# Opening part of a decoder trunk: adapter mixes in one VectorE operation, later splits on VectorE, three squares and six roundings on ScalarE

## The chip, the core and the metric

One core of one Trainium2 chip runs the whole kernel. The metric is device time of one execution in microseconds (us). Names of engines as the profile has them: PE is TensorE's matmul stream (PEld its weight loads), DVE is VectorE, ACT is ScalarE, POOL is GpSimd, SP is SyncE, which issues the loads. In the profile, L513 is line 513 of the kernel before.

## What is computed

Two decoder layers on x of 512 tokens by 1024 channels. The opening part, which the change touches, belongs to the first layer:

```python
h = rms_norm(x, norm_g[l, 0])
xx = jnp.pad(x, ((0, 0), (1, 0), (0, 0)))[:, :-1] - x
xr, xw, xk, xv, xa, xg = [x + xx * mu[i] for i in range(6)]
r = xr @ w_rkv[0]
k = xk @ w_rkv[1]
w = -jax.nn.softplus(-(w_decay0 + jnp.tanh(xw @ w_decay1) @ w_decay2)) - 0.5
a = jax.nn.sigmoid(a0 + (xa @ a1) @ a2)
g = jax.nn.sigmoid(xg @ g1) @ g2
kk = heads(k * k_k)
kk = kk * lax.rsqrt(jnp.maximum(jnp.sum(kk * kk, axis=-1, keepdims=True), 1e-24))
```

After it come the recurrence, its output projection, a convolutional feed-forward, attention with a window of 128, and a second feed-forward.

## The kernel before

Channels lie on partitions: x is eight tiles of 128 channels by 512 tokens, often worked in two halves of 256. Large products run in three passes: a weight is rounded to a high part (`whi`) and the rest is kept as a low part (`wlo`), the input likewise (two tiles both named `h`), and PE adds high by high, high by low and low by high. So each operand needs a rounding (a cast) and a subtraction.

The opening is written out by hand. The string `START` is a list of steps; each word is a step's letter, its chunk and, where there is a choice, its engine (D is DVE, A is ACT, P is POOL). Each engine works its own steps in the order of the list, and a step waits for what it reads and for the buffer that it writes. Twelve buffers of 512 columns (`t2`) serve most of the steps. The steps that matter here, with their lines:

- `x` (L442): normalises a half chunk. `m`, `s` (L337, L342): its mix for k. `c`, `u` (L452, L455): high and low part of that mix; PE's products `a`, `b`, `k` and `C` (L473) read them.
- `h`, `l` (L463, L466): high and low part of a weight block of 128 by 1024.
- `d` (L508, L509): the difference to the token before, one tile of 512 columns for each chunk. From it come the mixes for r (number 0), the decay (1), the adapter of a (4) and the gate (5): either `M` (L513), one DVE operation (difference times mu plus x), or the pair `e` (L517, a scaling on ACT) and `f` (L520, an addition on POOL). Each chunk needs four; sixteen of the 32 go as `e` and `f`.
- `W` (L525) and `g` (L532): PE's products of the adapters and the gate, which read these mixes as fp32.
- `H`, `L` (L616, L619): high and low part of the mix for r.
- `o` (L491) and `y` (L494): k scaled by k_k, and k itself, out of PSUM. `z` (L499 on ACT, L501 on POOL): the square of the scaled k, into a single buffer `ksq`. `S` (L504): PE's sum of squares.
- `E` (L587 to L611): loads, roundings and low parts of the adapters' second weights, in two column halves. The roundings stand on DVE (L591, L598, L605), the subtractions on POOL (L593, L600, L607).

Later stages are put in order by a scheduler when the program is built. After about 113 us the opening's end follows (tables of ScalarE, the norm of k), then a loop over eight blocks of r.

Of the kernel before, what the change touches and what calls it, by code (L numbers as in the profile page):

```python
# [12 lines left out]
F32 = mybir.dt.float32  # L13
F32R = mybir.dt.float32r
U32 = mybir.dt.uint32
AF = mybir.ActivationFunctionType
ALU = mybir.AluOpType
# [10 lines left out]
VQ = 4  # L28
VP = 3
VY = 1  # L30
START = 'q00P q02A q03D G02 O +023D q01P G03 G00 G01 +002D +001D q06P q05A q07D G07 q04P G05 +067P G06 +045D h0A n0 G04 l0P q12D q10A q11D G10 q13D +101D t0 G11 v0 h1D T0 l1D +123P G12 r2 G13 B0 q14A x02P +102D q16A r3 1 q15A x07D x03P q17A x00D m02 +145D +167P m00 x01D s02 m03 +146P s00 m01 s03 x04P c02A n1 c00A c03A s01 x06D t1 c01A u03D u00P m07 u02P m04 v1 u01D T1 h2A x05P s04 a000 x10D a010 x11D h3A a020 l2P d0D a030 c04A M50 b000 m06 a021 s07 m11 b010 s06 m05 g0 s11 u04P c07A r4 G15 c06D u06D l3P c11A a001 s05 b020 G17 c05D a040 G14 u05D b030 e10 u11D x14D a031 m10 a112 x15D m14 x17D d1P a050 r5 u07D m15 s14 b040 m17 c14D a060 B1 s15 G16 f10 a070 u14D e11 a061 a071 s10 s17 b050 e41 f11 M40 b060 c17A b041 c15A c10D b021 u17D b112 e01 f41 u15D u10D b142 e00 e51 f51 b011 x16P a142 4 x13P a051 m16 a152 s16 x12P m13 a041 b152 c16A s13 d2P m12 c13D W0 u13D s12 c12D W1 u16P u12D e42 M12 d3P e02 a172 M52 b070 a122 f42 M43 e53 b061 e03 b122 f53 a011 a132 a162 f00 b102 f01 a102 b031 o0 y0D g1 f02 z0A h5D h4A b051 M13 W2 l5P y1A r6 b071 b172 d4P r7 b162 b132 o1 l4D b001 W3 d5P M14 e04 S0 2 E30 o2 y3D o3 g2 z1P k5 M44 y2A f03 E40 E50 f04 M54 e45 f45 W4 h6D o5 l6D S1 e15 E60 k4 z2P f15 E70 g3 E80 E00 h7D o4 y4A y5D r8 l7D g4 d6P E10 S2 E31 C0 z3A C1 E20 W5 H0A E01 L0P e46 M55 E41 f46 e16 S3 H1D C2 E11 E61 L1D z4A f16 C3 H2A E51 L2D C4 H3A M56 H4A M06 C5 M05 E71 d7P L3D E21 S4 C6 z5A H5D E81 M47 e57 L5D C7 f57 M17 H6D W6 L4D h8A y7D y6D M07 g5 l8P o7 o6 S5 H7D W7 z6A L7D S6 F4 g6 z7P F5 E9 L6P F0 S7 g7 N0 F1 F2 N1 F3 R0 5 J00 Z0 N2 R2 A00 Z1 V30 A01 V00 V20 V31 R1 V01 V10 V21 J10 Y V32 V11 J01 N3 V02 R3 V22 R5 X0 R4 N4 V12 N5 R6 X1 R7 J11'
FIRST = 'apib0c1drs'
RG0 = 0
RG1 = 1
# [42 lines left out]
class Net:  # L77
# [272 lines left out]
    def rwkv(self, after_pool):  # L350
        nc, tc, d, par = self.nc, self.tc, self.d, self.par
        X = self.X
# [17 lines left out]
        t2 = lambda name, dt=F32: pT.tile([128, T], dt, name=name, tag="t2")  # L370
        mu = par[:, PC["mu"]:PC["mu"] + 48]
# [8 lines left out]
        raws, W, P, R = {}, {}, {}, {}  # L380
        ss, pwa, pg = self.ps(), None, None
        sq, st, ms, mw, df, rsb = {}, {}, {}, {}, {}, {}
# [129 lines left out]
            mw[i, c] = t2("m")  # L512
            nc.vector.scalar_tensor_tensor(mw[i, c], df[c], mu[:, 8 * i + c:8 * i + c + 1], X[:, c], ALU.mult, ALU.add)  # L513

        def f_e(i, c):
            mw[i, c] = t2("m")
            nc.scalar.activation(mw[i, c], df[c], AF.Identity, scale=mu[:, 8 * i + c:8 * i + c + 1])  # L517

        def f_f(i, c):
            nc.gpsimd.tensor_tensor(mw[i, c], mw[i, c], X[:, c], ALU.add)  # L520

        def f_W(c):
            R["wa"] = pwa = R.get("wa") or self.ps()
            for i, x in enumerate((mw.pop((1, c)), mw.pop((4, c)))):
                nc.tensor.matmul(pwa[64 * i:64 * i + 64, :], one["wa1"][:, c, 64 * i:64 * i + 64], x, start=c == 0, stop=c == 7, skip_group_check=True)  # L525
# [58 lines left out]
        def f_E(i, n=0):  # L584
            ns = slice(n * T, n * T + T)
            A2, AL, W2, WL = (one[k] for k in ("A2", "AL", "W2", "WL"))
            if i == 0:  # L587
                R["a2"] = t2("a2r")
                nc.sync.dma_start(R["a2"], d["a2"][:, ns])
            elif i == 1:  # L590
                nc.vector.tensor_copy(A2[:, ns], R["a2"])  # L591
            elif i == 2:
                nc.gpsimd.tensor_tensor(AL[64:128, ns], R["a2"][64:128, :], A2[64:128, ns].bitcast(F32), ALU.subtract)  # L593
            elif i == 3:
                R["w2"] = t2("w2r")
                nc.sync.dma_start(R["w2"], d["w2"][:, ns])
            elif i == 4:
                nc.vector.tensor_copy(W2[:, ns], R["w2"])  # L598
            elif i == 5:
                nc.gpsimd.tensor_tensor(WL[0:64, ns], R["w2"][0:64, :], W2[0:64, ns].bitcast(F32), ALU.subtract)  # L600
            elif i == 6:
                R["w2l"] = t2("w2l")
                nc.sync.dma_start(R["w2l"], d["w2l"][:, ns])
            elif i == 7:
                nc.vector.tensor_copy(WL[64:128, ns], R["w2l"][64:128, :])  # L605
            elif i == 8:
                nc.gpsimd.tensor_tensor(WL[96:128, ns], R["w2l"][96:128, :], WL[96:128, ns].bitcast(F32), ALU.subtract)  # L607
            else:
                one0 = t2("one0")
                nc.gpsimd.memset(one0[64:128, :], 1.0)  # L610
                nc.vector.tensor_copy(one["TB"][64:128, :], one0[64:128, :])  # L611
# [84 lines left out]
        with tc.manual_schedule():  # L696
            for k in START.split():
                fs[k[0]](*(int(x) if x.isdigit() else x for x in k[1:]))
# [55 lines left out]
        for q in range(8):  # L754
# [6 lines left out]
            for n in range(4):  # L761
                ns = slice(n * 128, n * 128 + 128)
# [58 lines left out]
        E0, n0, s0 = self.inverse(0, sp0, sp0)  # L821
        E1, n1, s1 = self.inverse(1, pE, sp0)
# [734 lines left out]
```

## Time and profile before

| what | value |
|---|---|
| median of three runs | 1413.12 us (1409.84 to 1417.49) |
| profiled execution | 1420.08 us, span in the trace 1418.2 us |
| PE busy | 1335.7 us, 94% |
| DVE busy | 940.0 us, 66% |
| ACT busy | 653.3 us, 46% |
| POOL busy | 528.9 us, 37% |

Busy shares are means over stages with different limits. Times below are counted from the span's start. The granted clock (PEclk) is the share of TensorE's full speed: 1.00 is 2.4 GHz, 0.50 is 1.2 GHz.

### The profile page before, as it was taken

To read this page: it belongs to the slowest core of one execution; us is meant where nothing else is said; L and a number is where in the kernel's file an instruction comes from. 1 tells how busy PE (TensorE), PEld (TensorE's weight loads), DVE (VectorE), ACT (ScalarE), POOL (GpSimd) and SP (SyncE) were. 2 spreads that over 40 slices of the span, in tenths; PEclk is the share of its full clock that TensorE was granted. 3 is DMA by queue.
4 is the path that set the end of the run, shared out by engine and by line. 5 is a ranking of instruction groups with operands and counts; after the bars stand their busy time and mean duration, and the time that the engine had idled before them with its cause. 6 is when DMAs were issued, how large, how long until landed. Compare 5 with 4: busy or idle time off the path is not lost.

```text
span 1418.2 us, 26067 instructions
## 1 busy us (share of the span) xinstructions
PE 1335.7 (94%) x10840; PEld 1116.4 (79%) x10840; DVE 940.0 (66%) x1384; ACT 653.3 (46%) x1192; POOL 528.9 (37%) x335
## 2 busy tenths in 40 slices
PE   4889999877989999999999989999999999999996
PEld 4766778777889888888888989766888888888886
DVE  8787898764797497776612287886658777763214
ACT  6436541334666454434322467766635444433232
POOL 6773420002445244333312635424533343332144
PEclk9899999898999999999999989999999999999998
DMA  5122121002344223333233424212323233232333
GB/s 198 38 69 72 60 63 35 14 19 63 107 153 146 89 76 104 104 97 97 82 97 93 138 96 150 89 60 74 120 71 108 90 103 104 89 99 83 95 99 122
DMA packets 43591, 130.07 MB, mean 92 GB/s; under 512 B 4560, under 2 KB 12496, under 8 KB 43472
## 3 DMA queue, kind: packets, MB, share of 16 engines
q1 hardware_dynamic: 41072, 126.11, 28.4%
q10 hardware_dynamic: 2400, 2.29, 0.5%
q8 instruction: 85, 1.39, 0.4%
q14 instruction: 34, 0.28, 0.1%
HBM read 124.19 MB, written 2.10 MB: 89 GB/s over the span
## 4 chain that ended last, share of the span: by engine, by line
PE 63%; DVE 3%; ACT 1%; issue 1%; POOL 0%; DVEq 0%; ACTq 0%; POOLq 0%
PE ps L124 19%; PE ps L126 19%; PE ps L125 19%; PE ps L1394 2%; PE ps L1358 1%; PE ps L1357 1%; DVE h L198 1%; DVE X L210 1%; DVE wlo L107 1%; PE ps L1384 1%; ACT h L197 1%; DVE acc L173 0%; PE ps L154 0%; POOL wlo L107 0%; DVE yy L209 0%
## 5 line engine op out<-in xcount | busy, mean ns | idle before, releaser
L107 POOL TENSOR_TENSOR wlo<-raw,whi 128x1024 fp32r<-128x1024 f32 (+1 forms) x126 | 304.3, 2417 | 350.6 <-ACT whi L102 304.9
L102 ACT CAST whi<-raw 128x1024 fp32r<-128x1024 f32 (+1 forms) x215 | 219.5, 1025 | 333.8 <-PE ps L125 235.3
L125 PE MATMUL ps<-h,whi 128*128 128x512 f32 (+1 forms) x984 | 359.7, 366 | 3.0 <-DVE h L198 2.9
L126 PE MATMUL ps<-h,wlo 128*128 128x512 f32 (+1 forms) x984 | 359.5, 366 | 2.8 <-DVE wlo L107 1.8
L124 PE MATMUL ps<-h,whi 128*128 128x512 f32 (+1 forms) x984 | 360.1, 368 | 0.0
L107 DVE TENSOR_TENSOR wlo<-raw,whi 128x1024 fp32r<-128x1024 f32 (+1 forms) x89 | 117.9, 1325 | 174.2 <-ACT whi L102 174.0
L126 PEld LDWEIGHTS ps<-h,wlo 128*128 128x128 f32 x984 | 189.2, 192 | 34.8 <-DVE wlo L107 2.7
L125 PEld LDWEIGHTS ps<-h,whi 128*128 128x128 f32 x984 | 189.3, 192 | 34.0 <-DVE h L198 3.5
L124 PEld LDWEIGHTS ps<-h,whi 128*128 128x128 f32 x984 | 188.1, 192 | 33.8 <-issue 2.8
L125 PE MATMUL ps<-g,whi 128*128 128x512 f32 (+1 forms) x440 | 153.7, 349 | 0.0
L124 PE MATMUL ps<-g,whi 128*128 128x512 f32 (+1 forms) x440 | 153.4, 349 | 0.0
L126 PE MATMUL ps<-g,wlo 128*128 128x512 f32 (+1 forms) x440 | 153.4, 349 | 0.0
L303 POOL TENSOR_TENSOR cs<-cs 128x512 f32<-128x512 f32 x44 | 57.7, 1312 | 242.8 <-DVE cs L295 200.3
L143 DVE TENSOR_TENSOR g<-cs,g 128x512 fp32r<-128x512 f32 x44 | 93.9, 2134 | 40.8 <-ACT g L142 40.8
L173 DVE TENSOR_TENSOR acc<-acc,sq 128x256 f32<-128x256 f32 x56 | 48.8, 886 | 72.9 <-ACT sq L172 72.6
L124 PEld LDWEIGHTS ps<-g,whi 128*128 128x128 f32 x440 | 82.6, 188 | 12.2
L125 PEld LDWEIGHTS ps<-g,whi 128*128 128x128 f32 x440 | 82.6, 188 | 12.2
L126 PEld LDWEIGHTS ps<-g,wlo 128*128 128x128 f32 x440 | 82.6, 188 | 12.1
L302 ACT ACTIVATE cs<-cs 128x512 f32<-128x512 f32 x44 | 27.8, 632 | 120.8 <-DVE cs L295 120.8
L292 DVE TENSOR_TENSOR rp<-ps,rsx 128x512 f32<-128x512 f32 x88 | 59.7, 686 | 31.3 <-PE ps L126 31.3
L293 ACT ACTIVATE cs<-rp,par 128x512 f32<-128x512 f32 x88 | 70.3, 812 | 16.3 <-DVE g L143 8.6
L294 DVE SCALAR_TENSOR_TENSOR cs<-rp,par,cs 128x511 f32<-128x511 f32 x88 | 74.0, 847 | 1.9 <-ACT cs L293 1.9
(298 smaller groups left out, 2404.8 us busy)
## 6 DMA issues: line engine op xcount, KB each, us to landing
raw<-w_up SPq DMA_DIRECT2D x88, 512.0 KB, 3.5
raw<-w_down SPq DMA_DIRECT2D x40, 512.0 KB, 3.6
raw<-w_or SPq DMA_DIRECT2D x16, 512.0 KB, 3.7
raw<-w_q SPq DMA_DIRECT2D x16, 512.0 KB, 3.5
raw<-w_oa SPq DMA_DIRECT2D x16, 512.0 KB, 3.5
raw<-w_down SPq DMA_DIRECT2D x20, 384.0 KB, 3.2
raw<-w_k SPq DMA_DIRECT2D x8, 512.0 KB, 3.7
raw<-w_r SPq DMA_DIRECT2D x8, 512.0 KB, 3.7
```

The costliest lines, as they stand in the source:

```text
L102: (nc.vector.tensor_copy if lo and lo[-1] == "v" else nc.scalar.copy)(hi, raw)
L107: (nc.gpsimd if lo[0] == "P" else nc.vector).tensor_tensor(wl, raw, hi.bitcast(F32), ALU.subtract)
L124: mm(p, hi, ah, start=first, stop=False, skip_group_check=True)
L125: mm(p, hi, al, start=False, stop=False, skip_group_check=True)
L126: mm(p, lo, ah, start=False, stop=last, skip_group_check=True)
L143: self.nc.vector.tensor_tensor(lo, src, hi.bitcast(F32), ALU.subtract)
L173: (eng or nc.vector).tensor_tensor(acc[:, o:o + n], acc[:, o:o + n], sq, ALU.add)
L292: nc.vector.tensor_tensor(r, p, rsx, ALU.mult)
L293: nc.scalar.activation(c, r, AF.Identity, bias=par[:, cb:cb + 1], scale=par[:, cw + 88:cw + 89])
L294: nc.vector.scalar_tensor_tensor(c[:, 1:], r[:, :T - 1], par[:, cw + 44:cw + 45], c[:, 1:], ALU.mult, ALU.add)
L303: nc.gpsimd.tensor_tensor(cs[:, 0], cs[:, 0], cs[:, 1], ALU.mult)
L1394: self.nc.tensor.matmul(po[64 * h:64 * h + 64, :], self.V[:, n - o, 64 * kvh:64 * kvh + 64], pt[:, o].rearrange("a i q -> a (i q)"), start ...
```

## The change

Sixteen mixes leave the pair `e` (ACT) and `f` (POOL) and become `M` (DVE), each at the place in the list where its `f` stood. Two low parts of weights (`l5`, `l8`) and two of the mix for r (`L0`, `L6`) go from POOL to DVE. Three squares (`z1`, `z2`, `z7`) go from POOL to ACT. In `E` the six roundings go from DVE to ACT, the six subtractions from POOL to DVE. SP's loads keep their order.

```diff
-b020 G17 c05D a040 G14 u05D b030 e10 u11D x14D a031
+b020 G17 c05D a040 G14 u05D b030 u11D x14D a031
...
-G16 f10 a070 u14D e11 a061 a071 s10 s17 b050 e41 f11 M40
+G16 M10 a070 u14D a061 a071 s10 s17 b050 M11 M40
...
-l5P
+l5D
...
-        def f_e(i, c):
-            mw[i, c] = t2("m")
-            nc.scalar.activation(mw[i, c], df[c], AF.Identity, scale=mu[:, 8 * i + c:8 * i + c + 1])
-
-        def f_f(i, c):
-            nc.gpsimd.tensor_tensor(mw[i, c], mw[i, c], X[:, c], ALU.add)
-
...
-                nc.vector.tensor_copy(A2[:, ns], R["a2"])
+                nc.scalar.copy(A2[:, ns], R["a2"])
             elif i == 2:
-                nc.gpsimd.tensor_tensor(AL[64:128, ns], R["a2"][64:128, :], A2[64:128, ns].bitcast(F32), ALU.subtract)
+                nc.vector.tensor_tensor(AL[64:128, ns], R["a2"][64:128, :], A2[64:128, ns].bitcast(F32), ALU.subtract)
...
```

The other two pairs of `E` change in the same way. Line numbers of the changed kernel are 7 lower from L520 on.

POOL, from the difference of chunk 1 to the half chunks 6, 3 and 2 of the second half of the tokens (L442). Before:

```order
L508 TENSOR_TENSOR df<-X 128x511
L509 TENSOR_SCALAR df<-X 128x1
L520 TENSOR_TENSOR m<-m,X 128x512 x4
L442 TENSOR_TENSOR X<-X,rsb 128x256 x3
L508 TENSOR_TENSOR df<-X 128x511
```

After:

```order
L508 TENSOR_TENSOR df<-X 128x511
L509 TENSOR_SCALAR df<-X 128x1
L442 TENSOR_TENSOR X<-X,rsb 128x256 x3
L508 TENSOR_TENSOR df<-X 128x511
L509 TENSOR_SCALAR df<-X 128x1
```

The four additions that stood ahead of the three normalisations are gone.

DVE in the same stretch, around the low parts of the k mix (L455). Before:

```order
L455 TENSOR_TENSOR h<-m,h 128x256
L342 SCALAR_TENSOR_TENSOR m<-X,par,m 128x256 x2
L513 SCALAR_TENSOR_TENSOR m<-df,par,X 128x512
L452 CAST h<-m 128x256
L455 TENSOR_TENSOR h<-m,h 128x256 x3
L650 TENSOR_SCALAR hpar<-par 128x8
```

After:

```order
L513 SCALAR_TENSOR_TENSOR m<-df,par,X 128x512
L455 TENSOR_TENSOR h<-m,h 128x256
L342 SCALAR_TENSOR_TENSOR m<-X,par,m 128x256 x2
L513 SCALAR_TENSOR_TENSOR m<-df,par,X 128x512 x2
L452 CAST h<-m 128x256
L455 TENSOR_TENSOR h<-m,h 128x256
L513 SCALAR_TENSOR_TENSOR m<-df,par,X 128x512
L455 TENSOR_TENSOR h<-m,h 128x256 x2
L513 SCALAR_TENSOR_TENSOR m<-df,par,X 128x512
L643 TENSOR_SCALAR hpar<-par 128x8
```

Four mixes have come in, three of them ahead of the second of the three low parts.

DVE at the end of the products of k, up to the last two copies of k out of PSUM (L494). Before:

```order
L605 CAST WL<-w2l 64x512
L619 TENSOR_TENSOR h<-m,h 128x512
L616 CAST h<-m 128x512
L513 SCALAR_TENSOR_TENSOR m<-df,par,X 128x512
L619 TENSOR_TENSOR h<-m,h 128x512
L513 SCALAR_TENSOR_TENSOR m<-df,par,X 128x512
L616 CAST h<-m 128x512
L619 TENSOR_TENSOR h<-m,h 128x512
L494 COPY bk<-ps 128x8x64 x2
L513 SCALAR_TENSOR_TENSOR m<-df,par,X 128x512
```

After (L609 is the cast and L612 the subtraction of the mix for r, L600 a subtraction of `E`):

```order
L609 CAST h<-m 128x512
L600 TENSOR_TENSOR WL<-w2l,WL 32x512
L513 SCALAR_TENSOR_TENSOR m<-df,par,X 128x512
L612 TENSOR_TENSOR h<-m,h 128x512
L513 SCALAR_TENSOR_TENSOR m<-df,par,X 128x512 x2
L609 CAST h<-m 128x512
L612 TENSOR_TENSOR h<-m,h 128x512
L494 COPY bk<-ps 128x8x64 x2
L513 SCALAR_TENSOR_TENSOR m<-df,par,X 128x512
```

The two copies keep their place behind the mixes of the last chunks; one more mix stands ahead of them.

## Rows read from the trace of the kernel before

**Rows 1.** The page, busy time: us, share of the span, instructions of each engine.

```profile
PE 1335.7 (94%) x10840; PEld 1116.4 (79%) x10840; DVE 940.0 (66%) x1384; ACT 653.3 (46%) x1192; POOL 528.9 (37%) x335
```

**Rows 2.** PE in order of time: start, us, operation [idle before, who ended it].

```profile
51.07 0.42 PE L473 MATMUL ps<-h,whi 128*128 128x256 f32 x1 [2.90 <-DVE h L452]
52.47 0.58 PE L473 MATMUL ps<-h,whi 128*128 128x256 f32 x1 [0.98 <-DVE h L455]
...
105.61 1.73 PE L525 MATMUL ps<-m,wa 128*64 128x512 f32 x4 [4.06 <-DVE m L513]
109.13 2.08 PE L504 MATMUL ps<-ksq,cst 128*128 128x512 f32 x2 [1.78 <-ACT ksq L499]
111.00 2.10 PE L532 MATMUL ps<-g,m 128*128 128x160 f32 x8
```

**Rows 3.** Stretches: us, busy time and (instructions) by engine, granted clock, DMA, GB/s.

```profile
35.40:106.40 71.00, 63.05 (x327) 48.19 (x326) 56.51 (x59) 27.38 (x45) 53.67 (x43) 0.93 0.17 54
51.30:58.10 6.80, 5.82 (x27) 5.63 (x27) 6.18 (x4) 0.72 (x1) 5.63 (x4) 0.50 0.00 0
105.90:112.70 6.80, 5.02 (x13) 2.54 (x10) 5.31 (x8) 5.12 (x8) 1.35 (x2) 0.50 0.55 162
120.00:180.00 60.00, 60.00 (x273) 45.44 (x271) 48.05 (x58) 32.05 (x52) 28.74 (x23) 1.00 0.19 60
180.00:240.00 60.00, 57.97 (x937) 45.48 (x939) 57.22 (x103) 20.05 (x29) 7.45 (x6) 1.00 0.16 48
```

**Rows 4.** DVE by line, 35.4 to 106.4: busy us, mean ns | idle before, releasers.

```profile
L513 DVE SCALAR_TENSOR_TENSOR m<-df,par,X 128x512 f32<-128x512 f32 x14 | 19.4, 1408 | 4.6 <-POOL h L619 3.5 <-POOL df L509 1.1
L466 DVE TENSOR_TENSOR wlo<-raw,whi 128x1024 fp32r<-128x1024 f32 x3 | 9.2, 3078 | 0.1
L342 DVE SCALAR_TENSOR_TENSOR m<-X,par,m 128x256 f32<-128x256 f32 x7 | 5.3, 765 | 2.8 <-ACT m L337 2.8
...
L455 DVE TENSOR_TENSOR h<-m,h 128x256 fp32r<-128x256 f32 x7 | 4.4, 650 | 0.1
...
L452 DVE CAST h<-m 128x256 fp32r<-128x256 f32 x4 | 3.0, 748 | 0.1
...
L494 DVE COPY bk<-ps 128x512 f32<-128x512 f32 x3 | 2.0, 682 | 2.8 <-ACT ar L491 2.8
L598 DVE CAST W<-w2r 128x512 fp32r<-128x512 f32 x2 | 1.9, 974 | 1.4 <-DMA w2r<-w 1.4
...
L605 DVE CAST WL<-w2l 64x512 fp32r<-64x512 f32 x2 | 1.6, 788 | 0.1
```

**Rows 5.** DVE in order of time, where POOL did little; columns as in rows 2.

```profile
36.37 0.29 DVE L452 CAST h<-m 128x256 fp32r<-128x256 f32 x1
36.58 0.48 DVE L342 SCALAR_TENSOR_TENSOR m<-X,par,m 128x256 f32<-128x256 f32 x1
...
41.06 1.08 DVE L455 TENSOR_TENSOR h<-m,h 128x256 fp32r<-128x256 f32 x3
...
94.06 2.07 DVE L513 SCALAR_TENSOR_TENSOR m<-df,par,X 128x512 f32<-128x512 f32 x3
...
108.28 1.21 DVE L107 TENSOR_TENSOR wlo<-raw,whi 128x1024 fp32r<-128x1024 f32 x1
```

**Rows 6.** POOL by line, 35.4 to 106.4; columns as in rows 4.

```profile
L520 POOL TENSOR_TENSOR m<-m,X 128x512 f32<-128x512 f32 x16 | 23.3, 1474 | 6.3 <-ACT m L517 6.2
L508 POOL TENSOR_TENSOR df<-X 128x511 f32<-128x511 f32 x6 | 8.2, 1371 | 3.0 <-DVE m L513 2.9
...
L509 POOL TENSOR_SCALAR df<-X 128x1 f32<-128x1 f32 x6 | 3.0, 504 | 0.0
...
L442 POOL TENSOR_TENSOR X<-X,rsb 128x256 f32<-128x256 f32 x3 | 2.4, 819 | 0.0
```

**Rows 7.** ACT in order of time, between the last copies of k and their squares' sum.

```profile
107.13 1.29 ACT L491 ACTIVATE ar<-ps,par 128x512 f32<-128x512 f32 x2 [6.40 <-DVE bk L494]
108.45 0.63 ACT L499 ACTIVATE ksq<-ar 128x512 f32<-128x512 f32 x1
```

More of the change, by code (lines that the diff above doesn't have):

```diff
@@ L30 @@
 VY = 1
-START = 'q00P q02A q03D G02 O +023D q01P G03 G00 G01 +002D +001D q06P q05A q07D G07 q04P G05 +067P G06 +045D h0A n0 G04 l0P q12D q10A q11D G10 q13D +101D t0 G11 v0 h1D T0 l1D +123P G12 r2 G13 B0 q14A x02P +102D q16A r3 1 q15A x07D x03P q17A x00D m02 +145D +167P m00 x01D s02 m03 +146P s00 m01 s03 x04P c02A n1 c00A c03A s01 x06D t1 c01A u03D u00P m07 u02P m04 v1 u01D T1 h2A x05P s04 a000 x10D a010 x11D h3A a020 l2P d0D a030 c04A M50 b000 m06 a021 s07 m11 b010 s06 m05 g0 s11 u04P c07A r4 G15 c06D u06D l3P c11A a001 s05 b020 G17 c05D a040 G14 u05D b030 e10 u11D x14D a031 m10 a112 x15D m14 x17D d1P a050 r5 u07D m15 s14 b040 m17 c14D a060 B1 s15 G16 f10 a070 u14D e11 a061 a071 s10 s17 b050 e41 f11 M40 b060 c17A b041 c15A c10D b021 u17D b112 e01 f41 u15D u10D b142 e00 e51 f51 b011 x16P a142 4 x13P a051 m16 a152 s16 x12P m13 a041 b152 c16A s13 d2P m12 c13D W0 u13D s12 c12D W1 u16P u12D e42 M12 d3P e02 a172 M52 b070 a122 f42 M43 e53 b061 e03 b122 f53 a011 a132 a162 f00 b102 f01 a102 b031 o0 y0D g1 f02 z0A h5D h4A b051 M13 W2 l5P y1A r6 b071 b172 d4P r7 b162 b132 o1 l4D b001 W3 d5P M14 e04 S0 2 E30 o2 y3D o3 g2 z1P k5 M44 y2A f03 E40 E50 f04 M54 e45 f45 W4 h6D o5 l6D S1 e15 E60 k4 z2P f15 E70 g3 E80 E00 h7D o4 y4A y5D r8 l7D g4 d6P E10 S2 E31 C0 z3A C1 E20 W5 H0A E01 L0P e46 M55 E41 f46 e16 S3 H1D C2 E11 E61 L1D z4A f16 C3 H2A E51 L2D C4 H3A M56 H4A M06 C5 M05 E71 d7P L3D E21 S4 C6 z5A H5D E81 M47 e57 L5D C7 f57 M17 H6D W6 L4D h8A y7D y6D M07 g5 l8P o7 o6 S5 H7D W7 z6A L7D S6 F4 g6 z7P F5 E9 L6P F0 S7 g7 N0 F1 F2 N1 F3 R0 5 J00 Z0 N2 R2 A00 Z1 V30 A01 V00 V20 V31 R1 V01 V10 V21 J10 Y V32 V11 J01 N3 V02 R3 V22 R5 X0 R4 N4 V12 N5 R6 X1 R7 J11'
@@ new lines @@
+START = 'q00P q02A q03D G02 O +023D q01P G03 G00 G01 +002D +001D q06P q05A q07D G07 q04P G05 +067P G06 +045D h0A n0 G04 l0P q12D q10A q11D G10 q13D +101D t0 G11 v0 h1D T0 l1D +123P G12 r2 G13 B0 q14A x02P +102D q16A r3 1 q15A x07D x03P q17A x00D m02 +145D +167P m00 x01D s02 m03 +146P s00 m01 s03 x04P c02A n1 c00A c03A s01 x06D t1 c01A u03D u00P m07 u02P m04 v1 u01D T1 h2A x05P s04 a000 x10D a010 x11D h3A a020 l2P d0D a030 c04A M50 b000 m06 a021 s07 m11 b010 s06 m05 g0 s11 u04P c07A r4 G15 c06D u06D l3P c11A a001 s05 b020 G17 c05D a040 G14 u05D b030 u11D x14D a031 m10 a112 x15D m14 x17D d1P a050 r5 u07D m15 s14 b040 m17 c14D a060 B1 s15 G16 M10 a070 u14D a061 a071 s10 s17 b050 M11 M40 b060 c17A b041 c15A c10D b021 u17D b112 M41 u15D u10D b142 M51 b011 x16P a142 4 x13P a051 m16 a152 s16 x12P m13 a041 b152 c16A s13 d2P m12 c13D W0 u13D s12 c12D W1 u16P u12D M12 d3P a172 M52 b070 a122 M42 M43 b061 b122 M53 a011 a132 a162 M00 b102 M01 a102 b031 o0 y0D g1 M02 z0A h5D h4A b051 M13 W2 l5D y1A r6 b071 b172 d4P r7 b162 b132 o1 l4D b001 W3 d5P M14 S0 2 E30 o2 y3D o3 g2 z1A k5 M44 y2A M03 E40 E50 M04 M54 M45 W4 h6D o5 l6D S1 E60 k4 z2A M15 E70 g3 E80 E00 h7D o4 y4A y5D r8 l7D g4 d6P E10 S2 E31 C0 z3A C1 E20 W5 H0A E01 L0D M55 E41 M46 S3 H1D C2 E11 E61 L1D z4A M16 C3 H2A E51 L2D C4 H3A M56 H4A M06 C5 M05 E71 d7P L3D E21 S4 C6 z5A H5D E81 M47 L5D C7 M57 M17 H6D W6 L4D h8A y7D y6D M07 g5 l8D o7 o6 S5 H7D W7 z6A L7D S6 F4 g6 z7A F5 E9 L6D F0 S7 g7 N0 F1 F2 N1 F3 R0 5 J00 Z0 N2 R2 A00 Z1 V30 A01 V00 V20 V31 R1 V01 V10 V21 J10 Y V32 V11 J01 N3 V02 R3 V22 R5 X0 R4 N4 V12 N5 R6 X1 R7 J11'
@@ L597, in f_E @@
             elif i == 4:
-                nc.vector.tensor_copy(W2[:, ns], R["w2"])
+                nc.scalar.copy(W2[:, ns], R["w2"])
             elif i == 5:
-                nc.gpsimd.tensor_tensor(WL[0:64, ns], R["w2"][0:64, :], W2[0:64, ns].bitcast(F32), ALU.subtract)
+                nc.vector.tensor_tensor(WL[0:64, ns], R["w2"][0:64, :], W2[0:64, ns].bitcast(F32), ALU.subtract)
             elif i == 6:
@@ L604, in f_E @@
             elif i == 7:
-                nc.vector.tensor_copy(WL[64:128, ns], R["w2l"][64:128, :])
+                nc.scalar.copy(WL[64:128, ns], R["w2l"][64:128, :])
             elif i == 8:
-                nc.gpsimd.tensor_tensor(WL[96:128, ns], R["w2l"][96:128, :], WL[96:128, ns].bitcast(F32), ALU.subtract)
+                nc.vector.tensor_tensor(WL[96:128, ns], R["w2l"][96:128, :], WL[96:128, ns].bitcast(F32), ALU.subtract)
             else:
```

## The prediction

> **What bounds the kernel now.** I read the page first: PE is busy 94% of the span [rows 1], so a gain has to come from PE's idle time or from its slow clock. The chain of work that ended last doesn't reach back to the opening, so there I read PE in order of time and looked at who ended each idle piece. From 120 us to 180 us PE is busy for all of 60 us, and from 180 us to 240 us for 57.97 [rows 3]: what the opening saves is passed on by these stages. In the opening PE stops in three places after its start. The first, near 33 us, lies ahead of the first step that moves. The second is 2.90 + 0.98 us, for DVE's high and low part of the k mix (L452, L455). The third is 4.06 us for a mix (L513) and 1.78 us for the last but one square (L499) [rows 2]. After the second and the third the granted clock is 0.50, the lower of TensorE's two levels (1.2 GHz of 2.4): 5.82 us and 5.02 us of PE's work were done in that state [rows 3] and would take half at full clock, so it costs 2.9 and 2.5 us. All that PE can get back is 2.90 + 0.98 + 4.06 + 1.78 + 2.9 + 2.5 = **15.1 us**.
>
> DVE is the engine PE waits for, and DVE is late because of POOL. In 35.4 to 106.4 DVE is busy 56.51 of 71.0 us [rows 3], but the same operation takes different times. A mix (L513) takes 2.07 / 3 = 0.69 us where POOL is nearly idle [rows 5] and 1.41 us in the mean [rows 4]; a low part of a weight 1.21 against 3.08. The copy that reads PSUM (L494) has a mean of 0.68 and shows no such spread [rows 4]. So operations with all operands in SBUF wait inside their own time for POOL. What this costs in the stretch, mean rows [rows 4] against free rows [rows 5]: mixes 19.4 - 14 x 0.69 = 9.7; weight low parts 9.2 - 3 x 1.21 = 5.6; k mixes (L342) 5.3 - 7 x 0.48 = 1.9; low parts (L455) 4.4 - 7 x 0.36 = 1.9; casts (L452) 3.0 - 4 x 0.29 = 1.8. Together **20.9 us**.
>
> **The change part by part, on DVE, up to its two copies of k at 106.42** (the wait on DVE's L494 in [rows 7]). Added: sixteen mixes at 0.69 are 11.0 us; one weight low part 1.2 (the other stands behind the copies); six subtractions of `E` and one low part for r (the other also stands behind) at the mix's 0.69, 4.8. Removed: six casts of `E`; L598's pair took 1.9, L605's 1.6 [rows 4], and the third pair, of L598's shape, as much as that: 5.4. Net **+11.6 us** of work.
>
> What POOL keeps in the stretch: six differences, 8.2 + 3.0, and three normalisations, 2.4 [rows 6], with one low part of about 0.8 (a normalisation's mean) 14.4 of its 53.67 us [rows 3], or 27%. If DVE's waits shrink with POOL's work, 73% of 20.9 goes, **-15.3 us**. DVE's idle time for POOL, 3.5 + 1.1 [rows 4], goes too, **-4.6**: the low part that it waited for is now its own or comes from an emptier POOL. The idle time for PE, ACT, DMA stays as it is. The sum is 11.6 - 15.3 - 4.6 = **-8.3 us** at the copies.
>
> Behind the copies stands a chain that doesn't change: two scalings on ACT (1.29), the square (0.63), then PE's sum of squares at 109.13 [rows 7, 2]. PE must be there too: without its stops and the slow clock after 51 it comes 2.90 + 0.98 + 2.9 + 4.06 + 1.78 = 12.6 us earlier. It gets one new stop: three added mixes stand ahead of the second of three low parts (at 41.06 before [rows 5]), 2.1 us, and the three normalisations, which now run beside them, can hold DVE 2.4 us more. Up to 4.3 us of this the DVE chain hides, 12.6 - 8.3; all of it would be 4.5. So DVE decides, at -8.3.
>
> Then the clock. The sum of squares and the gate's products after it take 2.08 and 2.10 us at 0.50 [rows 2]; with PE's idle time before them cut to under 3 us I expect full clock, -2 us. Bounds: 0 and -2.5.
>
> At no cost: ACT loses sixteen scalings and gets three squares and six casts, and it is busy 27.38 of 71.0 us [rows 3]. A square on ACT takes 0.63 [rows 7], and `ksq`, a single buffer, is free as soon as PE has read it. The casts of `E` are first read after 113 us. If ACT's cover fails, each late square costs PE up to 0.6. POOL gets nothing. SP's queue is the same, and loads follow buffers that come free earlier. Some rows of later stages change places by one or two; I take 0, bounds -1 and +1.
>
> The sum: -8.3 - 2 = -10.3, taken as **-10 us**. The profiled execution took 1420.08, of which 1418.2 is the span: it becomes 1410. It lies 7 us above the median of the runs shown; the stops of the opening are no reason for that difference, so the same step is taken from the median: 1413.1 - 10 = **1403**.
>
> **What the notes say of it.** L513 takes 0.69 or 1.41 as POOL is idle or busy, L494 always 0.68 [rows 4, 5]. The Trainium skill, SBUF — State Buffer, Who interferes with whom, says that a VectorE instruction with two SBUF inputs, and casts in the two-port modes, share a port pair with GpSimd, that the one that starts first holds it for its whole instruction, and that one with at most one SBUF input outside these modes doesn't contend: the trace agrees on L494. The rule weighs against a part of my sum, since by it every POOL operation that is left can hold DVE for its full time (rival 2). The Trainium skill, Perfetto Trace Analysis, Optimizing Scalar/DVE Operations, says that a saturated VectorE is a reason to move work off it, even to GpSimd, and adds that their common port may make this useless. This change does the opposite (rival 3).
>
> **The rivals.**
> 1. *All of it.* DVE's loss goes wholly and its 2.8 us for the mixes behind POOL's normalisations too: 11.6 - 20.9 - 4.6 - 2.8 = -16.7 at the copies, which is more than PE can use. PE is the bound and saves its 15.1: 1398. For it: the sixteen additions, 23.3 us of POOL's time [rows 6], go, and the normalisations come right behind a difference. Against: six differences stay. 0.12.
> 2. *What POOL keeps holds DVE fully.* Each of its 14.4 us is then lost on DVE, so only 20.9 - 14.4 = 6.5 goes: 11.6 - 6.5 - 4.6 = +0.5, no gain at the copies; perhaps 3 us at the second stop and its clock. In between lies a mixed case with half of this, about -5: 1408 to 1412. Against: before, 53.67 us of POOL cost 20.9, or 0.39 for each us, which makes 5.6 of 14.4. For: DVE has fewer gaps now, so that POOL's operations more often meet one. 0.20.
> 3. *DVE becomes the bound, slower.* If the long times are not POOL's doing, nothing of 20.9 goes: 11.6 - 4.6 = +7.0 at the copies, and PE's longer stop at 105 us adds one more piece of slow clock, 2: +9, or 1422. It decides as soon as less than a third (7.0 us) of the loss goes. Against: L494 and the free rows. 0.06.
> 4. *The gain doesn't arrive.* From 180 us to 240 us DVE is busy 57.22 of 60 [rows 3] and PE can't go ahead of it. But DVE comes there earlier too, since its own queue is what got shorter; DMA's share there is 0.16. Price -2 or so: 1411. 0.04.
>
> **How the numbers follow.** My forecast has 0.58, with -7 to -13 (the part of the loss that goes between 0.65 and 0.9, the clock between 0 and -2.5): 1400 to 1406. A measurement of this kernel can tell about 0.5%, 7 us, from no change. Faster by more than that: nearly all of the forecast, rival 1 and a little of rival 2, 0.71. Within it: most of rival 2, rival 4, a rest of the forecast, 0.23. Slower: rival 3, 0.06. The range is **1397 to 1412**: it leaves out the far end of rival 1 and rival 3, and part of rival 2.
>
> **What the profile after would show.** Mixes (L513) with a mean near 0.8 instead of 1.41, weight low parts near 1.3; DVE busy some 50 to 53 us up to its copies of k, and these at about 98. PE's stop at 51 us gone or under 1 us, one of 1 to 3 us near 43 us, the 4.06 us for the mix gone, 1 to 3 us left for the square, the clock 1.00 around the third place. The loop over r starts 10 us earlier and everything after it is shifted by as much. I am wrong if the mixes stay above 1.1 us, if PE waits for a mix at all in the third place, or if the shift is there at 120 us and not at 240.

## The result and the profile after

The kernel after takes **1398.8 us** (median of 6 runs, 1394.94 to 1407.97), the kernel before took 1415.78 on the same chip: ratio 0.990, 95% interval 0.986 to 0.993. Timed twice more in later sessions it took 1403.4 (10 runs; before 1413.6; 0.992, 0.989 to 0.996) and 1404.7 (6 runs; before 1416.9; 0.991, 0.987 to 0.994). Forecast were 1403 and 10 us less than before; measured are 17.0, 10.2 and 12.2 us less. The profiled execution took 1400.81 us, its span is 1398.9.

The page, busy time by engine, answering [rows 1]:

```profile
PE 1322.9 (95%) x10840; PEld 1104.3 (79%) x10840; DVE 934.7 (67%) x1404; ACT 647.6 (46%) x1185; POOL 488.2 (35%) x306
```

What ended PE's idle time from 24 us to 125 us: engine, line, us in total, times, longest:

```profile
PE ps L473 <- DVE h L455: 1.4, 1, 1.4
PE ps L473 <- ACT h L452: 1.3, 1, 1.3
PE ps L504 <- ACT ksq L499: 1.0, 1, 1.0
...
```

The first two are the stop near 33 us, ahead of the change. The stops at 51 us and at 105 us [rows 2] are gone; of the third place only the wait for the square is left. There PE in order of time (start, us, operation [idle before, who ended it]), then ACT ([rows 7] before):

```profile
96.09 1.08 PE L518 MATMUL ps<-m,wa 128*64 128x512 f32 x4
98.17 1.12 PE L504 MATMUL ps<-ksq,cst 128*128 128x512 f32 x2 [1.00 <-ACT ksq L499]
99.13 1.25 PE L525 MATMUL ps<-g,m 128*128 128x160 f32 x8
```

```profile
96.17 1.29 ACT L491 ACTIVATE ar<-ps,par 128x512 f32<-128x512 f32 x2 [2.05 <-DVE bk L494]
97.49 0.63 ACT L499 ACTIVATE ksq<-ar 128x512 f32<-128x512 f32 x1
```

L518 is L525 of before: the adapter's products no longer wait for a mix. The scalings, the square and the sum of squares all stand 10.96 us earlier (107.13, 108.45, 109.13 before). The sum takes 1.12 us instead of 2.08, the gate's products 1.25 instead of 2.10.

Stretches (us, busy and instructions of PE, PEld, DVE, ACT, POOL, then the granted clock, DMA, GB/s). The first goes up to DVE's last two copies of k, so that it answers the 71.0 us of [rows 3]; the last answers 180 us to 240 us there, since this work now stands some 11 us earlier:

```profile
35.40:95.40 60.00, 60.00 (x323) 46.93 (x323) 49.98 (x77) 21.99 (x39) 16.82 (x17) 0.95 0.19 62
34.20:45.00 10.80, 10.30 (x63) 10.30 (x64) 10.77 (x22) 3.50 (x9) 5.65 (x5) 0.69 0.01 3
170.00:230.00 60.00, 58.00 (x945) 44.85 (x944) 55.66 (x102) 18.52 (x26) 6.29 (x5) 0.97 0.16 47
```

DVE does more instructions in less time: 77 in 49.98 us against 59 in 56.51. Where this comes from, DVE by line from 35.4 to 95.4 (busy us, mean ns | idle before, releaser), against [rows 4]:

```profile
L513 DVE SCALAR_TENSOR_TENSOR m<-df,par,X 128x512 f32<-128x512 f32 x30 | 22.0, 770 | 0.0
L466 DVE TENSOR_TENSOR wlo<-raw,whi 128x1024 fp32r<-128x1024 f32 x4 | 5.6, 1427 | 0.1
L342 DVE SCALAR_TENSOR_TENSOR m<-X,par,m 128x256 f32<-128x256 f32 x7 | 4.9, 723 | 0.0
L612 DVE TENSOR_TENSOR h<-m,h 128x512 fp32r<-128x512 f32 x6 | 4.1, 688 | 2.7 <-ACT h L609 2.6
L455 DVE TENSOR_TENSOR h<-m,h 128x256 fp32r<-128x256 f32 x7 | 3.8, 553 | 0.1
...
L586 DVE TENSOR_TENSOR AL<-a2r,A 64x512 fp32r<-64x512 f32 x2 | 2.1, 1054 | 0.1
...
L600 DVE TENSOR_TENSOR WL<-w2l,WL 32x512 fp32r<-32x512 f32 x2 | 1.4, 689 | 0.2
L593 DVE TENSOR_TENSOR WL<-w2r,W 64x512 fp32r<-64x512 f32 x2 | 1.4, 682 | 3.5 <-ACT W L591 3.5
L609 DVE CAST h<-m 128x512 fp32r<-128x512 f32 x3 | 1.3, 421 | 0.0
L452 DVE CAST h<-m 128x256 fp32r<-128x256 f32 x4 | 1.2, 291 | 0.1
...
```

Thirty mixes take 22.0 us where fourteen took 19.4. How far the opening as a whole moved is seen at its last product of r (L473). One row has all matmuls of a line: ns min/median/max, the first and the last start in us. Before, then after:

```profile
L473 PE MATMUL ps<-h,whi x206: 278/389/799, 23.6 to 123.5; 128*128 128x256 f32 x63, 128*128 128x512 f32 x40
```

```profile
L473 PE MATMUL ps<-h,whi x206: 279/389/799, 23.7 to 111.0; 128*128 128x256 f32 x63, 128*128 128x512 f32 x40
```

The **last start of L473**, 123.5 and 111.0, is the mark used below: the opening is 12.5 us shorter.

### The profile page after: what moved, and what is told of

It is laid out like the page before. It is cut to its first block, busy times and chain, and to the rows that moved or that the text cites. A ratio compares the mean times of both kernels' runs of the same rounds, so it can differ in the third digit from the quotient of the medians.

```text
span 1398.9 us, 26032 instructions
## 1 busy us (share of the span) xinstructions
PE 1322.9 (95%) x10840; PEld 1104.3 (79%) x10840; DVE 934.7 (67%) x1404; ACT 647.6 (46%) x1185; POOL 488.2 (35%) x306
## 4 chain that ended last, share of the span: by engine, by line
PE 64%; DVE 4%; issue 1%; ACT 1%; POOL 0%; DVEq 0%; ACTq 0%; POOLq 0%
PE ps L124 19%; PE ps L126 19%; PE ps L125 19%; PE ps L1387 2%; PE ps L1351 1%; PE ps L1350 1%; DVE h L198 1%; DVE X L210 1%; DVE wlo L107 1%; PE ps L1377 1%; DVE acc L173 0%; PE ps L154 0%; POOL wlo L107 0%; DVE yy L209 0%; PE ps L1205 0%
## 5 line engine op out<-in xcount | busy, mean ns | idle before, releaser
L126 PEld LDWEIGHTS ps<-h,wlo 128*128 128x128 f32 x984 | 186.3, 189 | 35.1 <-DVE wlo L107 2.7
L125 PEld LDWEIGHTS ps<-h,whi 128*128 128x128 f32 x984 | 186.3, 189 | 33.8 <-DVE h L198 3.4
L124 PEld LDWEIGHTS ps<-h,whi 128*128 128x128 f32 x984 | 184.9, 189 | 34.0 <-issue 2.7
L125 PEld LDWEIGHTS ps<-g,whi 128*128 128x128 f32 x440 | 82.6, 188 | 12.2
L124 PEld LDWEIGHTS ps<-g,whi 128*128 128x128 f32 x440 | 82.6, 188 | 12.2
```

What stands on the lines that cost most here:

```text
L124: mm(p, hi, ah, start=first, stop=False, skip_group_check=True)
L125: mm(p, hi, al, start=False, stop=False, skip_group_check=True)
L126: mm(p, lo, ah, start=False, stop=last, skip_group_check=True)
```

## Experiments

Theory A: while GpSimd reads SBUF, VectorE's operations on SBUF take longer; the change gains what it takes off GpSimd's reading. Theory B: the gain is in the hand-overs between ScalarE, GpSimd and VectorE that a mix in one operation does without.

### The two parts alone

`mixes_only` is the kernel before with the sixteen mixes alone; `rest_only` is the kernel before with all the rest alone.

```diff
mixes_only, in START, and so on for sixteen mixes:
-... b030 e10 u11D ... G16 f10 a070 u14D e11 ... b050 e41 f11 M40 ...
+... b030 u11D ... G16 M10 a070 u14D ... b050 M11 M40 ...
rest_only, in START, and the twelve operations of E as in the change:
-... l5P ... z1P ... z2P ... L0P ... l8P ... z7P ... L6P ...
+... l5D ... z1A ... z2A ... L0D ... l8D ... z7A ... L6D ...
```

> The kernel before with the first part of the change alone: sixteen mixes in one VectorE operation; splits, squares and roundings stay as before. Port theory: GpSimd loses 23.3 of its 53.7 us in the stretch up to the last copies of k, VectorE gets 11.0 us of work and loses 0.43 x 20.9 = 9.1 us of waiting, so the copies hardly move by this sum, but PE's stop at 51 us goes with its slow clock: 2 to 6 us by 190 us. Rival (hand-over): nearly all of the gain is here, 9 to 12 us.

> The kernel before with the rest of the change alone: four low parts and six subtractions on VectorE, three squares and six roundings on ScalarE; the sixteen mixes keep their pair of a scaling and an addition. Port theory: GpSimd loses 16 us, VectorE's work grows by 0.6 us net, its waits shrink by 0.3 x 20.9 = 6.3 and its idle time for GpSimd by 4.6: the stop at 51 us stays, the one at 105 us shrinks, 5 to 9 us by 190 us. Rival (hand-over of the mixes): 0 to 3 us.

Measured: mixes_only 1406.75 us, ratio 0.996 (0.993 to 0.998), last start of L473 115.4; rest_only 1404.2 us, 0.993 (0.991 to 0.996), 115.7. Each alone gives 8 us in the opening (8.1 and 7.8), 15.9 in sum, together 12.5. For rest_only that is what Theory A forecast, and the stop at 51 us stayed as it said. For mixes_only both forecasts missed: 8.1 lies between the 2 to 6 us of Theory A and the 9 to 12 of Theory B. Why the sum exceeds the whole can be seen in part in what PE waits for from 24 us to 125 us; mixes_only first, then rest_only:

```profile
...
PE ps L504 <- ACT ksq L499: 2.4, 1, 2.4
PE ps L525 <- DVE m L513: 1.9, 1, 1.9
...
```

```profile
PE ps L473 <- DVE h L452: 2.7, 1, 2.7
...
PE ps L504 <- ACT ksq L499: 1.5, 1, 1.5
...
```

Both parts shorten the stop of 4.06 us for a mix: the mixes alone leave 1.9 of it, the rest alone nothing. So 2.2 us of this stop are counted twice in the sum; the other 1.2 us are not taken apart. The stop at 51 us goes with the mixes alone (2.7 us of it stay in rest_only). In mixes_only the mean of a mix is 0.928 us, in rest_only 1.219: GpSimd keeps work in both.

### GpSimd reads, or GpSimd is only busy

To the kernel after, sixteen operations on GpSimd are added where the sixteen additions stood; they write a buffer that nobody uses. In `pad_read` each is an add of 128 x 512 that reads x. In `pad_write` each is a pair of memsets of 128 x 512, which read nothing.

```diff
 in START, sixteen times
-... G16 M10 a070 ...
+... G16 M10 p0 a070 ...
 pad_read
+        def f_p(c):
+            nc.gpsimd.tensor_tensor(one["pad"], X[:, c], X[:, c], ALU.add)
 pad_write
+        def f_p(c):
+            for _ in range(2):
+                nc.gpsimd.memset(one["pad"], 1.0)
```

> The changed kernel with sixteen extra GpSimd additions of 128x512, each at the place where an addition of the old pair stood: they read x and write a buffer that nobody reads, so no engine waits for their result. Port theory (VectorE operations with all operands in SBUF wait while GpSimd reads SBUF): VectorE's mixes go back to a mean over 1.2 us, PE stops again near 50 us and 100 us, and of the 12 us that the opening gained by 190 us at most 3 are left. Rival (the gain is the shorter hand-over, since no mix goes from ScalarE to GpSimd any more): the mixes keep some 0.8 us and at least 8 of the 12 us stay.

> As pad_read, but each extra addition is replaced by two GpSimd memsets of 128x512, about as long together (0.52 us each by the memset of the trace, against 1.03 for an addition that waits for nobody). Port theory, as the page on SBUF has it (two SBUF inputs wait only for a GpSimd operation that reads): mixes stay near 0.7 to 0.9 us, 9 to 13 of the 12 us stay. If what counts is that GpSimd's queue is held up (normalisations and differences come late), it loses as much as pad_read. If a GpSimd operation of any kind blocks VectorE, likewise, with mixes over 1.2 us.

Measured: pad_read 1405.92 us, ratio 0.996 (0.993 to 0.999), last start of L473 117.1; pad_write 1399.93, 0.991 (0.988 to 0.994), 111.9. pad_write came as Theory A forecast. For pad_read neither forecast was met: 6.4 of the 12.5 us stay, where Theory A had at most 3 and Theory B at least 8, and the mixes take 0.975 us, between its "over 1.2" and 0.8. From 35.4 us to 95.4 us, columns as above, pad_read and then pad_write:

```profile
35.40:95.40 60.00, 55.64 (x300) 44.01 (x300) 55.32 (x75) 19.88 (x36) 31.02 (x28) 0.93 0.20 62
```

```profile
35.40:95.40 60.00, 58.19 (x321) 44.60 (x322) 50.26 (x78) 22.50 (x39) 30.45 (x45) 1.00 0.19 62
```

POOL is as busy in both, 31.02 and 30.45 us. DVE is busy 55.32 us with 75 instructions where POOL reads, and 50.26 with 78 where it only writes; the kernel after has 49.98 with 77. The mixes from 35.4 us to 106.4 us, again pad_read first:

```profile
L513 DVE SCALAR_TENSOR_TENSOR m<-df,par,X 128x512 f32<-128x512 f32 x31 | 29.1, 975 | 0.0
```

```profile
L513 DVE SCALAR_TENSOR_TENSOR m<-df,par,X 128x512 f32<-128x512 f32 x31 | 23.2, 783 | 0.0
```

The Trainium skill, SBUF — State Buffer, Who interferes with whom, says that a VectorE instruction with two SBUF inputs contends with a GpSimd instruction that reads SBUF, and not with one that only writes it. This pair of runs agrees: 0.975 against 0.783 us, and 0.769 without either (a row of the last section).

The plainest place is the first four additions. POOL's row of them, then PE's first wait for DVE behind them, in pad_read:

```profile
32.18 4.72 POOL L516 TENSOR_TENSOR pad<-X 128x512 f32<-128x512 f32 x4
...
37.90 0.58 PE L473 MATMUL ps<-h,whi 128*128 128x256 f32 x1 [4.50 <-DVE h L455]
```

The same in pad_write:

```profile
32.78 4.65 POOL L517 MEMSET pad<- 128x512 f32 x8
...
35.49 0.38 PE L473 MATMUL ps<-h,whi 128*128 128x256 f32 x1 [1.46 <-DVE h L455]
```

POOL is busy at the same time and for as long, yet PE's stop is 4.50 us beside reads and 1.46 beside writes (1.4 in the kernel after).

So GpSimd's busy time alone costs little: pad_write's opening ends 0.9 to 1.7 us later than those of the kernel after. But pad_read takes back only 6.1 of the 12.5 us, and 3.1 us of this is the longer stop near 38 us, which the kernel before doesn't have (1.4 us there). So half of the gain or more could still be Theory B's. That needed the third kernel.

### All that was taken off GpSimd, put back as reading

`pad_all` adds to the kernel after an add of 128 x 512 wherever the change took an operation off GpSimd, 29 places, two adds for each of the two weight low parts.

```diff
 in START, twenty-nine times
-... l5D y1A ... M11 M40 ... z2A M15 ...
+... l5D p02 y1A ... M11 p11 M40 ... z2A p01 M15 p51 ...
+        def f_p(c, n):
+            for k in range(n):
+                nc.gpsimd.tensor_tensor(one["pad"], X[:, c + k], X[:, c + k], ALU.add)
```

> The kernel after, with an extra GpSimd add (128 x 512, reads X, writes an unused buffer) wherever the change took an operation off GpSimd: 29 places, two adds for each of the two 128 x 1024 parts, 31 adds. The 16 adds alone (pad_read) gave 6.0 of the 12.4 us back by 190 us. Theory A, the price is GpSimd reading at the same time as VectorE: the other 15 adds give back more; the same matmuls at 190 us stand 3 to 8 us later than in pad_read, that is between 3 us before and 2 us behind the kernel before; mixes mean 0.98 to 1.15 us, ratio to before 0.997 to 1.003. Theory B, the mixes gain because no hand-over between ScalarE, GpSimd and VectorE is left, and GpSimd's reading costs only what pad_read showed: 190 us stays near 6 us earlier than before, ratio near 0.996, as pad_read.

Measured: 1418.91 us, ratio 1.002 (0.998 to 1.005): the whole gain is gone. Its L473, its mixes, what PE waits for (L522 has the adapters' products there), and the stretch that answers the first one of [rows 3]:

```profile
L473 PE MATMUL ps<-h,whi x208: 277/389/799, 23.7 to 127.1; 128*128 128x256 f32 x64, 128*128 128x512 f32 x40
```

```profile
L513 DVE SCALAR_TENSOR_TENSOR m<-df,par,X 128x512 f32<-128x512 f32 x29 | 33.9, 1202 | 0.0
```

```profile
PE ps L522 <- DVE m L513: 6.4, 2, 3.3
PE ps L473 <- DVE h L455: 4.8, 2, 4.5
PE ps L504 <- ACT ksq L499: 3.3, 1, 3.3
...
```

```profile
35.40:106.40 71.00, 63.48 (x325) 48.86 (x325) 67.20 (x80) 22.50 (x39) 50.50 (x42) 0.91 0.17 53
```

Every mix is one operation and no hand-over is back, yet the opening ends 3.6 us later than before (127.1 against 123.5). So the hand-overs aren't what the gain rests on, and Theory B falls; that they had a small share in it isn't excluded. Of Theory A's forecasts for this run the ratio came true; the mixes were slower than forecast (1.202 us against 1.15 at most) and the overshoot was larger (2 us at most).

Two things in the trace point at the overshoot. GpSimd is busy nearly as long as before (50.50 us of 71, before 53.67), but VectorE still has the work that the change gave it: it is busy 67.20 us against 56.51. And the added operations wait for nothing, where the additions that they stand for waited for a scaling: the first four run without a break from 32.61 us on, before the first came at 34.34 and the next at 37.55, and PE's stop of 4.50 us near 38 us is the one of pad_read. How the 3.6 us divide between the two isn't shown.

### Taking more off GpSimd

`l23_dve` is the kernel after with two weight low parts (`l2`, `l3`) on VectorE. `more_dve` has these, all the differences `d` and five half-tile operations (`x`, `u`) on VectorE, and the last two copies of k (`y`) on ScalarE.

```diff
 l23_dve, in START
-... l2P ... l3P ...
+... l2D ... l3D ...
 more_dve, in START
-... x04P ... l2P ... u04P ... l3P ... d1P ... x16P ... x13P ... x12P ... d2P ... d7P ... y7D y6D ...
+... x04D ... l2D ... u04D ... l3D ... d1D ... x16D ... x13D ... x12D ... d2D ... d7D ... y7A y6A ...
```

> The kernel after, with the rest of the reading work of GpSimd between 24 and 112 us moved to VectorE (the differences d1 to d7, the low parts l2 and l3, five half-tile products) and the last two copies of k (y6, y7) on ScalarE. Before 24 us nothing changes. Theory A, GpSimd's reading is the price: VectorE gets the 11 or so us of work at its own prices (differences 0.8 instead of 1.46 us on GpSimd, low parts 1.3 instead of 2.67) and its own operations come down to 0.70 for a mix; the stops of 1.4 and 1.3 us near 33 us and the slow clock behind them go, the square's 1.0 too: 2 to 6 us below the kernel after, ratio to before 0.985 to 0.989. Theory B, VectorE (9.96 us busy of 10 from 20 to 30 us, 9.86 of 10 from 30 to 40) is by now the bound of this part, so that 11 us more work on it makes TensorE wait near 45 to 60 us: 0 to 6 us slower than the kernel after, ratio 0.990 to 0.995.

> The same kernel as more_dve, timed in more rounds beside the kernel after. In more_dve's trace the matmuls at 190 us stood 17.3 us before those of the kernel before, 4.8 us earlier than in the profiled kernel after (4.0 earlier than in after_again). If that opening is what the time keeps: median 3 to 7 us below that of the kernel after on the same chip, ratio to before 0.986 to 0.990. If later parts give it back (rival): within 2 us of the kernel after.

> The kernel after with one difference: the low parts of the adapters' base weights l2 and l3 (128 x 1024, two operations of 2.67 us on GpSimd between 30 and 46 us) on VectorE, where five others took 1.385 each. If GpSimd's reading there is what slows VectorE's operations ahead of the stops near 33 us (1.4 and 1.3 us) and what follows, the matmuls at 60 us stand 1 to 3.5 us earlier than in the kernel after, of which more_dve had 3.6; if VectorE's full queue there is the limit (9.86 of 10 us busy), 2.8 us more on it push them 1 to 3 us later.

Measured: more_dve 1399.89 us (ratio 0.988, 0.983 to 0.993) beside 1403.41 for the kernel after, more_dve_long 1402.41 (0.988, 0.985 to 0.991) beside 1404.65. The last start of L473 is 106.2 and 106.7, against 111.0, 110.2 and 110.9 in the three profiles of the kernel after: 4 us earlier. In time it is 3.5 and 2.2 us, the second below the 3 to 7 us that were forecast, and the intervals overlap. So the trace shows a shorter opening; that the kernel is faster than the one after isn't shown. DVE in more_dve from 35.4 us to 106.4 us:

```profile
L513 DVE SCALAR_TENSOR_TENSOR m<-df,par,X 128x512 f32<-128x512 f32 x31 | 22.0, 743 | 0.0
L466 DVE TENSOR_TENSOR wlo<-raw,whi 128x1024 fp32r<-128x1024 f32 x5 | 6.1, 1218 | 0.1
...
```

The weight low part is back at the free 1.21 us of [rows 5], and six differences take 4.6 us that took 9.0 on POOL. PE waits for no square any more; near 32 us it still stops for 1.0 us, which the forecast had gone. So VectorE could take this work although it was busy 9.86 of 10 us from 30 us to 40 us: part of that time had been GpSimd's doing. l23_dve ran once (1390.21 us), with the last start of L473 at 109.8, 1.2 us or less ahead of the kernel after. Its products near 60 us were 1.3 to 2.1 us ahead, as expected, and most of it was lost again behind. The rest of its low time lies behind the opening, where the next section finds that one kernel's executions differ; a single run can't say more.

### What lies behind the opening

In the first profiled pair the difference grows from 12.5 us at the opening's end to 19.6 at the last matmul of L154, near the program's end. Part of this could be the change's, since the scheduler had put some rows of later stages in another order. So both kernels were profiled again.

> The kernel before, as it is. Theory A (the clock of one execution makes the later difference): its stretches at a clock below 1.00 after 250 us are not all those of the first profiled execution (829.5, 846.6, 897.8, 972.9, 1030.9), and the matmuls from 825 us on stand elsewhere by 2 us or more, up to 8; the opening up to 190 us stands within 1.5 us. Theory B (the change): the same stretches, all matmuls within 1.5 us of the first execution up to the end.

> The kernel after, as it is. Theory A, what lies between the two kernels beyond the 12.4 us of the opening (7 us more from 825 us on in the profiled pair) is the granted clock of the one execution: in this execution the opening stands again 11.5 to 13 us before that of the kernel before at 190 us, and the difference from 825 us to the end is another one than 7 us. Theory B, it is the change (a few instructions stand in another order there): the end again stands 18 to 20 us before that of the profiled kernel before, with the same stretches at a clock below 1.00.

> The kernel after, timed in more rounds: the opening's 12.4 to 13.3 us against a base of 1413 to 1416 us gives a ratio of 0.990 to 0.992, if nothing but the opening differs; 0.987 or below if the 7 us more from 825 us on, which one profiled pair showed, belonged to the change.

L154 sums squares for the norms between stages, far behind the opening; its last matmul is near the program's end. Before, before_again, after, after_again:

```profile
L154 PE MATMUL ps<-io,acc x56: 164/250/373, 425.8 to 1407.5; 128*128 128x1 f32 x56
```

```profile
L154 PE MATMUL ps<-io,acc x56: 164/250/271, 424.2 to 1399.3; 128*128 128x1 f32 x56
```

```profile
L154 PE MATMUL ps<-io,acc x56: 167/250/272, 414.8 to 1387.9; 128*128 128x1 f32 x56
```

```profile
L154 PE MATMUL ps<-io,acc x56: 164/250/371, 413.5 to 1395.7; 128*128 128x1 f32 x56
```

From the first to the last of them the same kernel before takes 981.7 and 975.1 us, the kernel after 973.1 and 982.2 (and 982.0 in after_long). Executions of one kernel differ as much as the two kernels do, so nothing here puts the 8.6 us more of the first pair down to the change. The ratio of after_long, 0.991, is also the one forecast for the opening alone, though its interval is wide. In the first pair the granted clock is the same from 240 us to 825 us (0.96 in both) and from 1060 us to 1385 us (1.00 in both). It differs from 825 us to 1060 us: PE busy, its instructions, clock, DMA, GB/s, in the same order of runs:

```profile
825.00:1060.00 235.00, 226.61 (x1458) 0.94 0.28 89
```

```profile
825.00:1060.00 235.00, 226.39 (x1482) 0.98 0.29 96
```

```profile
825.00:1060.00 235.00, 228.64 (x1486) 0.99 0.30 96
```

```profile
825.00:1060.00 235.00, 228.64 (x1456) 0.96 0.28 91
```

PE's busy time is nearly the same; the clock is 0.94 or 0.98 for one kernel and 0.99 or 0.96 for the other. What decides it in an execution stays open. The opening doesn't vary like this: its end stands at 111.0, 110.2 and 110.9 in three executions of the kernel after, at 123.5 and 123.3 in two of the kernel before.

## Why the prediction was right, step by step

- **The sum.** Forecast -10.3 for the opening; measured -12.5, -13.3 and -12.6 against the first profile of before. In time, -10.2 and -12.2 in the two later sessions and -17.0 in the first. That one is more than the 15.1 us that PE could get back in the opening at all, so part of it must lie behind; executions of one kernel differ there by 7 to 9 us. The first median, 1398.8, lies in the range 1397 to 1412.
- **DVE decides at its copies of k.** Right: copies, scalings, square and sum of squares moved by the same 10.96 us, as a chain that starts from DVE.
- **DVE's sum, -8.3.** Mis-sized: -11.0 (71.0 us became 60.0). Idle time was forecast at -4.6 and came at -4.5, but made up otherwise. The waits for POOL (4.6), for ACT's scaling L337 (2.8), for the load of `E` (1.4) and part of that for L491 went, and two new ones came: 3.5 us for the rounding L591 that the change had moved to ACT, and 2.6 for the rounding L609. Behind the first still stands a load of `E`: ACT itself had waited 2.44 us for it (the row below). The prediction had the roundings of `E` read only after 113 us; the subtractions on DVE read them at once, and whatever stands behind these in DVE's queue waits too. Of the second, 2.17 us lie at the first low part for r, which the change had moved from POOL to DVE: the prediction took that wait as gone. The total came out right by luck, because the errors cancelled. Busy time was forecast at 11.6 - 15.3 = -3.7 and came at 49.98 - 56.51 = -6.5.

```profile
66.87 0.62 ACT L591 CAST W<-w2r 128x512 fp32r<-128x512 f32 x1 [2.44 <-DMA w2r<-w]
```

- **The port loss, "73% goes".** Nearly right: by the same free durations, the lines that had 20.9 us of loss have 22.0 - 30 x 0.69 = 1.3, 5.6 - 4 x 1.21 = 0.8, 4.9 - 7 x 0.48 = 1.5, 3.8 - 7 x 0.36 = 1.3 and 0.0 left, 4.9 us: 77% is gone. The missing part is a term that the list of losses left out, r's own operations: its low parts had a mean of 0.895 us and its casts 0.778 before, and have 0.688 and 0.421 now. 5 x 0.207 + 3 x 0.357 = 2.1 us. The low parts of `E` were 0.8 us dearer than forecast (L586 takes 1.05), and operations on DVE overlap more (the lines' busy times sum to 3.0 us above DVE's before, 3.8 after). 0.7 + 2.1 - 0.8 + 0.8 = 2.8, the difference of the two sums.
- **The stops.** The one at 51 us gone, the 4.06 us gone, 1.00 us left for the square: right. The new one near 43 us isn't in the first profile after, since PE ran at a clock of 0.69 from 34.2 us to 45 us (0.84 before in the same stretch, the row below) and didn't get ahead of DVE. after_again, with a clock of 1.00 there, shows it as forecast, 1 to 3 us, and a remnant of the stop at 51 us. The stretch of before, then PE of after_again in order of time:

```profile
34.20:45.00 10.80, 10.44 (x75) 10.30 (x77) 8.20 (x20) 6.78 (x14) 6.78 (x6) 0.84 0.01 3
```

```profile
42.79 0.39 PE L473 MATMUL ps<-h,whi 128*128 128x256 f32 x1 [1.17 <-DVE h L455]
...
48.28 0.84 PE L473 MATMUL ps<-h,whi 128*128 128x256 f32 x2 [0.43 <-DVE h L452]
```

- **The clock, -2.** The sum of squares and the gate's products gave back 2.08 - 1.12 and 2.10 - 1.25, together 1.8 us; the clock there is 1.00. Right, though its premise, full clock after less than 3 us of idle time, doesn't hold everywhere: near 33 us PE stopped for 1.3 and 1.4 us in three executions of the kernel after, and from 34.2 us to 45 us the granted clock was 0.69, 1.00 and 0.84.
- **Later stages, 0.** Right as far as the runs can tell: the first matmul of L154 stands 11.0, 12.3 and 13.7 us earlier (412.1 in after_long), and what comes behind varies as much from one execution to the next of the same kernel. The stage in which DVE is nearly always busy only moved: from 170 us to 230 us PE is busy 58.00 us and DVE 55.66, where it was 57.97 and 57.22 from 180 us to 240 us before.
- **The rivals.** Rival 1 (all of the loss goes, 15.1 us on PE) was missed by 2.6 us. Rival 2 (what POOL keeps holds DVE fully) fell: POOL kept 16.82 us, and 4.9 us were lost on the lines listed, 0.3 for each. Rivals 3 and 4 didn't come; pad_all shows rival 3's condition from the other side, a mix in one operation on DVE while GpSimd goes on reading, and its ratio is 1.002.

## What to carry to other kernels

Before you judge whether a busy VectorE can take more work, compare the mean of one operation in the crowded stretch with the same operation where GpSimd is idle. If it takes twice as long, part of its busy time is waiting, and taking GpSimd's reading work over can shorten VectorE's queue even though its instructions grow. List that loss for every line of the stretch, not only for those that the change touches, and test it with a dummy operation on the other engine, once reading and once only writing.

## What the runs showed of the hardware

- For the mixes only GpSimd's reading counted. With POOL busy for the same 31 us a mix took 0.975 us beside adds and 0.783 beside memsets. For casts writing counted too, in the few places where the two met: in pad_write one cast for r (L613 there) took 0.78 us beside two memsets at 91.3 us, and the other three 0.42.
- The price was about the same in two runs: the mixes lost (29.1 - 22.7) / 18.8 = 0.34 us for each us of added reading in pad_read, and (33.9 - 29 x 22.7 / 31) / 35.6 = 0.36 in pad_all. The mixes of the kernel after from 35.4 us to 106.4 us, then the added operations of pad_read and of pad_all there:

```profile
L513 DVE SCALAR_TENSOR_TENSOR m<-df,par,X 128x512 f32<-128x512 f32 x31 | 22.7, 769 | 0.0
```

```profile
L516 POOL TENSOR_TENSOR pad<-X 128x512 f32<-128x512 f32 x14 | 18.8, 1344 | 0.8
```

```profile
L517 POOL TENSOR_TENSOR pad<-X 128x512 f32<-128x512 f32 x26 | 35.6, 1370 | 1.7
```

- The granted clock of a stretch isn't a property of the kernel: between 825 us and 1060 us it was 0.94 and 0.98 in two executions of the kernel before, and from the first to the last matmul of L154 these took 981.7 and 975.1 us. A difference of that size in a stage that the change doesn't touch needs a second profile of both kernels before it gets a reason.
